# A norm over 64 rows as two products with a block of ones, in place of column sums and turns

## The chip, the cores and the metric

The kernel runs on one core of a Trainium2 chip. The metric is the device time of one execution in microseconds: 2410.14 us for the kernel before (median of 3 runs, 2409.24 to 2412.32). The core's engines work side by side, each on its own queue in order: TensorE (PE, matrix products into PSUM), VectorE (DVE), ScalarE (ACT), GpSimd (POOL) and SyncE (SP, which starts the DMAs).

## The reference

A decoder trunk of two layers on 512 positions of width 1024. A layer is: half a SwiGLU feed-forward step, a mixer, a cross-attention to a memory of 256 positions, another half feed-forward step. All in float32. The mixer has two groups of heads side by side: 8 stick-breaking attention heads of width 64, and 4 gated DeltaNet heads of width 128. What the change touches is the norm of each attention head's output, over its 64 channels:

```
sb = stick_breaking_attention(sq, sk, sv)             # (B, 8 heads, 512, 64)
sb = rms_norm(sb, sb_out_norm.reshape(8, 1, 64))      # x * rsqrt(mean(x*x) + 1e-6) * gain
...
return concatenate([sb, go]) @ w_out
```

## The kernel before

**Layout and precision.** Activations lie with channels on the 128 partitions and the 512 positions along the free axis. A product in the type fp32r takes one pass over its columns but rounds its operands, so the dense products are made of three: each operand is split into a high part (a cast on ACT, `split_act`, L177) and a low part (a subtraction on DVE, `split_low`, L182), and hi*hi, hi*lo and lo*hi are summed (`mm3`). Weights come as blocks of 128x1024 by SP's DMAs, four split blocks are held ahead. Products of plain fp32 operands are used where matrices are small.

**The threads of a mixer.** `mixer` writes four Python generators and `weave` merges them: the norm of the input, the DeltaNet heads (`mixer_gdn`, four heads one after another), the attention pairs (`mixer_sb`, `sb_pair` four times, two heads each), and the dense products (`mixer_dense`). The planner has a clock that grows with each matrix product by its estimated cost. A thread yields either a delay in ns, after which it may go on, or names of marks that must have been set and be due. Whenever several are ready, the first in the order above goes on, so the dense thread fills what the others leave. PE's instructions are issued exactly in the order so found; the other engines' order is made by the framework, with the DeltaNet heads' work at high priority. A delay costs nothing in itself: it only says how much other PE work is put between two steps, and PE waits if an operand is late.

**What orders the threads.** Dense projects pair p's queries, keys and values (`sb_project`) and sets the mark `sbp{p}`, due 2700 ns later; `sb_pair` p starts when it is due. Dense may start the projections of head 2 and 3 only after marks `q0` and `q1` (a head's recurrence has ended), those of pairs 2 and 3 only after `qk0` and `qk1` (a pair's scores of its second head are issued). After the fourth pair it projects the gates z, begins the memory's keys, and waits for `qk3`; further keys wait for `l3` (the last head's triangular solve) and `q3`; the output projection takes pair 3's operand when `sb3` is marked.

**A pair.** The values are turned (four 128x128 turns through PE, L776, with the identity) into PSUM bank b5, the only bank of the key "av". Then scores, weights and the values' products for its first head, 11000 ns of delay, and the same for its second. The values' products end in bank b5 too; ACT copies half of it (L956) and DVE adds (L957) into `o`, 128 rows of which the upper and lower 64 are one head each.

**The pair's norm.** ACT squares `o` (L959). After 3900 ns four fp32 products with the squares as the stationary operand and `bones` (128x2: ones on the rows of either head) as the moving one leave sums per position, 128 positions x 8 columns, in b5 (`col_sums`). DVE adds eps (L964), `rsqrt_log` makes exp(-0.5*ln x) on ACT and one Newton step on DVE, all on 8 columns, and DVE spreads each root over 64 columns (L968). After 4700 ns four turns bring this back to channels on partitions, again in b5, and DVE multiplies `o` by gain and root (L973). `sbp` of the next pair being due, the next pair's turns follow.

**The queries' copies.** `sb_project` keeps the queries' high part twice, on either half of the partitions; the second copy is a DVE copy of 64x512 (L851), twice a pair.

Of the kernel before, what the change touches and what calls it, by code (L numbers as in the profile page):

```python
# [19 lines left out]
F32 = mybir.dt.float32  # L20
F32R = mybir.dt.float32r
BF16 = mybir.dt.bfloat16
I32 = mybir.dt.int32
AF = mybir.ActivationFunctionType
ALU = mybir.AluOpType
PSUM = bass.MemoryType.PSUM

P = 128
# [12 lines left out]
EPS = 1e-6  # L41
# [8 lines left out]
G_F1, G_MX, G_XA, G_ME, G_F2, G_SB, G_GD, G_CV, G_AL, G_DT, G_LAYER = (  # L50
    0, 8, 16, 24, 32, 40, 44, 45, 93, 97, 101)
# [3 lines left out]
class Trunk:  # L55
# [59 lines left out]
    def mm(self, out, lhsT, rhs, **kw):  # L115
        r = rhs.dtype != F32
        n = 1
        for d in out.shape[1:]:
            n *= d
        self.clk += max(56.0 if rhs.dtype == BF16 else 107.0, n / 2.37) * (1 if r else 2)  # L120
        self.nc.tensor.matmul(out, lhsT, rhs, **kw)  # L121
# [711 lines left out]
    def sb_project(self, pair, x):  # L833


        nc = self.nc
        t4 = self.sb([P, 4, S], "qk", F32R, bufs=2)
        kk, qq = [t4[:, i, :] for i in range(2)], [t4[:, 2 + i, :] for i in range(2)]
        ql = self.ql[pair % 2]
        half = [slice(64 * i, 64 * i + 64) for i in range(2)]  # L840
        for j in range(2):
            ps = yield from self.project(x)
            tmp = self.slot("s12")
            nc.vector.scalar_tensor_tensor(out=tmp, in0=ps, scalar=0.125 if j == 0 else 1.0, in1=self.rb,
                                           op0=ALU.mult, op1=ALU.mult)
            dst = (qq, kk)[j]
            for i, r in enumerate(half):
                self.split_act(dst[i][r], tmp[r])
                self.split_low(ql[i][r] if j == 0 else kk[i][half[1 - i]], tmp[r], dst[i][r])
                if j == 0:  # L850
                    nc.vector.tensor_copy(qq[i][half[1 - i]], qq[i][r])  # L851
        if pair:
            yield (f"vt{pair - 1}",)
        ps = yield from self.project(x)
        self.vf = self.slot("s14")
        nc.vector.tensor_tensor(self.vf, ps, self.rb, op=ALU.mult)
        self.qk[pair] = kk, qq, ql
        self.mark(f"sbp{pair}", 2700.0)
# [6 lines left out]
    def sb_pair(self, layer, pair):  # L865


        nc = self.nc
        mm = self.mm
        t1s = ("s15", "s16", "s17")  # L870
        names = [f"s{i}" for i in range(22, 27)]
        yield (f"sbp{pair}",)
        b = self.bank("av", self.AV)
# [7 lines left out]
        kk, qq, ql = self.qk[pair]  # L881
# [54 lines left out]
        o = self.slot(("s0", "s1", "s13", "s37")[pair])  # L936
        for j in range(2):
# [7 lines left out]
            av = self.bank("av", self.AV)  # L945
            for s in range(NT):
                if j == 0 and s < 3:
                    yield from scores(1, s)
                    if s == 2:
# [5 lines left out]
            low = self.slot(self.turn("t1", t1s))  # L955
            nc.scalar.copy(low[own], av[other])  # L956
            nc.vector.tensor_tensor(o[own], av[own], low[own], op=ALU.add)  # L957
        sq = self.slot(self.turn("t1", t1s))
        nc.scalar.activation(sq, o, AF.Square)  # L959
        yield 3900.0  # L960
        b = self.bank("av", self.AV)
        self.col_sums(b, sq, self.bones, 2)
        ms = self.sb([P, 8], "sms", bufs=2)
        nc.vector.tensor_scalar(out=ms, in0=b[:, 0:8], scalar1=1.0 / 64, scalar2=EPS,  # L964
                                op0=ALU.mult, op1=ALU.add)
        r = self.rsqrt_log(ms, 8, "sn")
        wide = self.slot(self.turn("t1", t1s))
        nc.vector.tensor_copy(wide.rearrange("p (c d) -> p c d", d=64),  # L968
                              r.unsqueeze(2).to_broadcast([P, 8, 64]))
        yield 4700.0  # L970
        b = self.bank("av", self.AV)
        self.transposes(b, wide)
        nc.vector.scalar_tensor_tensor(out=o, in0=o, scalar=self.gain(layer, G_SB, pair), in1=b,  # L973
                                       op0=ALU.mult, op1=ALU.mult)
        self.sbo[pair] = o
        self.mark(f"sb{pair}", 17600.0)
# [601 lines left out]
```

## Time and profile before

| what | value |
|---|---|
| median of the runs | 2410.14 us |
| the profiled execution | 2411.89 us, its span 2410.1 us |
| mean granted TensorE clock | 0.996 |
| busy shares of the span | PE 99%, PE's weight loads 87%, DVE 73%, ACT 49%, POOL 0% |
| the two mixers | about 380 to 690 us and 1575 to 1880 us |

In the rows, PE is TensorE's products and PEld its weight loads, L121 is the line of `mm` (nearly all products) and L776 that of a turn. A matrix product's printed duration is modelled and overlaps the next one; the distance of two starts tells what one costs. What stands in square brackets is the engine's idle time just before the row and who ended it.

### The profile page before, as it was taken

The numbers are of one execution on the slowest core, as the hardware profiler recorded it, in microseconds if no ns is written. First come the engines' busy times: TensorE is split into PE (matmuls) and PEld (weight loads), VectorE is DVE, ScalarE is ACT, GpSimd is POOL, SyncE is SP. The second block draws the span as 40 slices with busy tenths as digits, with TensorE's granted clock in tenths as the row PEclk, the third lists the DMA queues.
The fourth block names the chain that finished last, engine by engine and source line by source line (L and its number), as shares of the span: only waits on it lengthen the run. The fifth ranks groups of instructions, "written<-read, shape, count | busy, mean of one in ns | idle before, by whom it ended". The sixth has DMA issues, their size and how long they took to land.

```text
span 2410.1 us, 35914 instructions
## 1 busy us (share of the span) xinstructions
PE 2376.2 (99%) x14320; PEld 2096.5 (87%) x14320; DVE 1763.6 (73%) x3121; ACT 1191.8 (49%) x2042; POOL 8.1 (0%) x19
## 2 busy tenths in 40 slices
PE   9999999999999999999999999999999999999998
PEld 7999987878888889898989999888788888899997
DVE  7767677888865577585786776689888655867765
ACT  5435355655644444353544444466666443444443
POOL 0000000000000000000000000000000000000000
PEclk9999999999999999999999999999999999999999
DMA  5324242112223123232323232311122322232322
GB/s 179 102 85 126 76 135 71 53 45 71 71 93 117 62 86 117 79 123 88 114 79 123 81 115 87 123 62 53 45 75 85 104 96 71 79 123 79 115 87 88
DMA packets 71416, 220.49 MB, mean 91 GB/s; under 512 B 7376, under 2 KB 18384, under 8 KB 71248
## 3 DMA queue, kind: packets, MB, share of 16 engines
q1 hardware_dynamic: 70816, 217.82, 27.8%
q8 instruction: 112, 1.84, 0.3%
q14 instruction: 56, 0.46, 0.1%
q10 hardware_dynamic: 432, 0.37, 0.1%
HBM read 216.07 MB, written 2.10 MB: 91 GB/s over the span
## 4 chain that ended last, share of the span: by engine, by line
PE 57%; DVE 3%; ACT 1%; issue 0%; DVEq 0%; ACTq 0%
PE b L121 57%; PE b L776 1%; DVE wlo L182 0%; DVE s L903 0%; DVE s L182 0%; DVE qkv L989 0%; DVE qk L182 0%; DVE s L705 0%; DVE s L905 0%; ACT whi L177 0%; ACT qk L177 0%; DVE qk L851 0%; DVE s L1086 0%; DVE s L1126 0%; DVE s L898 0%
## 5 line engine op out<-in xcount | busy, mean ns | idle before, releaser
L121 PE MATMUL b<-s,whi 128*128 128x256 f32 (+1 forms) x2818 | 648.9, 315 | 0.0
L177 ACT CAST whi<-wraw 128x1024 fp32r<-128x1024 f32 (+3 forms) x412 | 388.4, 954 | 478.2 <-PE b L121 408.1
L121 PE MATMUL b<-xh,whi 128*128 128x512 f32 (+1 forms) x1430 | 570.3, 399 | 1.4 <-DVE h L605 0.9
L182 DVE TENSOR_TENSOR wlo<-wraw,whi 128x1024 fp32r<-128x1024 f32 (+3 forms) x412 | 451.6, 1102 | 142.9 <-ACT whi L177 140.3
L121 PE MATMUL b<-xl,whi 128*128 128x512 f32 x1396 | 544.1, 390 | 0.2 <-DVE xl L311 0.2
L121 PEld LDWEIGHTS b<-s,whi 128*128 128x128 f32 x2818 | 468.5, 190 | 34.2
L121 PE MATMUL b<-s,wlo 128*128 128x256 f32 (+1 forms) x1426 | 449.9, 315 | 0.0
L121 PE MATMUL b<-xh,wlo 128*128 128x512 f32 x1106 | 432.4, 391 | 0.7 <-DVE wlo L182 0.7
L121 PEld LDWEIGHTS b<-xh,whi 128*128 128x128 f32 x1430 | 269.1, 188 | 51.8 <-ACT xh L179 1.3
L121 PEld LDWEIGHTS b<-xl,whi 128*128 128x128 f32 x1396 | 262.8, 188 | 49.3 <-DVE xl L182 0.9
L121 PEld LDWEIGHTS b<-s,wlo 128*128 128x128 f32 x1426 | 270.8, 190 | 17.7
L121 PEld LDWEIGHTS b<-xh,wlo 128*128 128x128 f32 x1106 | 207.6, 188 | 47.5 <-DVE wlo L182 2.6
L121 PE MATMUL b<-qk,whi 128*128 128x256 f32 (+1 forms) x1168 | 238.9, 289 | 0.0
L605 DVE SCALAR_TENSOR_TENSOR h<-b,h 128x512 f32<-128x512 f32 (+1 forms) x98 | 66.3, 680 | 173.5 <-PE b L121 173.5
L121 PEld LDWEIGHTS b<-qk,whi 128*128 128x128 f32 x1168 | 184.1, 191 | 2.4
L121 PE MATMUL b<-qkv,whi 128*128 128x256 f32 x900 | 180.0, 282 | 0.9 <-ACT s L562 0.9
L121 PE MATMUL b<-qk,wlo 128*128 128x256 f32 (+1 forms) x568 | 164.1, 289 | 0.0
L121 PEld LDWEIGHTS b<-qkv,whi 128*128 128x128 f32 x900 | 140.5, 190 | 1.3 <-ACT s L562 1.1
L177 ACT CAST whi<-vv 128x1024 fp32r<-128x1024 f32 x67 | 70.4, 1051 | 125.6 <-issue 71.4
L121 PE MATMUL b<-qkv,wlo 128*128 128x256 f32 x466 | 131.1, 281 | 0.0
L121 PE MATMUL b<-xl,wlo 128*128 128x512 f32 x290 | 112.4, 388 | 0.0
L121 PEld LDWEIGHTS b<-qk,wlo 128*128 128x128 f32 x568 | 108.5, 191 | 1.3
(300 smaller groups left out, 3283.5 us busy)
## 6 DMA issues: line engine op xcount, KB each, us to landing
wraw<-f2i SPq DMA_DIRECT2D x88, 512.0 KB, 3.6
wraw<-f1i SPq DMA_DIRECT2D x86, 512.0 KB, 3.7
wraw<-wi SPq DMA_DIRECT2D x56, 512.0 KB, 3.6
wraw<-f1o SPq DMA_DIRECT2D x32, 512.0 KB, 3.5
wraw<-xkv SPq DMA_DIRECT2D x32, 512.0 KB, 3.7
wraw<-f2o SPq DMA_DIRECT2D x32, 512.0 KB, 3.5
wraw<-wo SPq DMA_DIRECT2D x16, 512.0 KB, 3.7
wraw<-xq SPq DMA_DIRECT2D x16, 512.0 KB, 3.7
```

Of the source, the lines that this page charges most:

```text
L121: self.nc.tensor.matmul(out, lhsT, rhs, **kw)
L177: self.nc.scalar.copy(hi, src)
L182: return self.nc.vector.tensor_tensor(lo, src, hi.bitcast(F32), op=ALU.subtract)
L605: stt(out=h, in0=p, scalar=0.5, in1=h, op0=ALU.mult, op1=ALU.add)
L776: self.nc.tensor.transpose(out, src, self.ident[:src.shape[0], :src.shape[0]])
```

## The change

In `sb_project` the queries' second copy is made by ACT. In `sb_pair` the squares are split into a high and a low part like a dense operand. POOL spreads `bones` to a 128x128 matrix of ones on two diagonal 64x64 blocks (`heads`). After one delay of 5000 ns two fp32r products with `heads` as the stationary operand and the two parts as the moving one give the sum of each head's squares on all of its 64 rows at once, 128x512 in b5. Scaling and eps, logarithm, exponential and the Newton step then run on 128x512, and the last multiplication reads the root from SBUF. There are no turns back and no second delay. The seven new buffers come from the five slots s22 to s26 that the pair's weights rotate through ("sbs"), no longer from s15 to s17.

```diff
                 if j == 0:
-                    nc.vector.tensor_copy(qq[i][half[1 - i]], qq[i][r])
+                    nc.scalar.copy(qq[i][half[1 - i]], qq[i][r].bitcast(F32))
...
-        sq = self.slot(self.turn("t1", t1s))
+
+        room = lambda dt=F32: self.slot(self.turn("sbs", names), dt)
+        sq, hi, lo = room(), room(F32R), room(F32R)
         nc.scalar.activation(sq, o, AF.Square)
-        yield 3900.0
+        self.split_act(hi, sq)
+        heads = room(F32R)[:, :P]
+        nc.gpsimd.tensor_copy(heads.rearrange("p (a d) -> p a d", a=2), self.bones.unsqueeze(2).to_broadcast([P, 2, 64]))
+        self.split_low(lo, sq, hi)
+        yield 5000.0
         b = self.bank("av", self.AV)
-        self.col_sums(b, sq, self.bones, 2)
-        ms = self.sb([P, 8], "sms", bufs=2)
-        nc.vector.tensor_scalar(out=ms, in0=b[:, 0:8], scalar1=1.0 / 64, scalar2=EPS,
-                                op0=ALU.mult, op1=ALU.add)
-        r = self.rsqrt_log(ms, 8, "sn")
-        wide = self.slot(self.turn("t1", t1s))
-        nc.vector.tensor_copy(wide.rearrange("p (c d) -> p c d", d=64),
-                              r.unsqueeze(2).to_broadcast([P, 8, 64]))
-        yield 4700.0
-        b = self.bank("av", self.AV)
-        self.transposes(b, wide)
-        nc.vector.scalar_tensor_tensor(out=o, in0=o, scalar=self.gain(layer, G_SB, pair), in1=b,
+        mm(b, heads, hi, start=True, stop=False)
+        mm(b, heads, lo, start=False, stop=True)
+        ms, r, t = room(), room(), room()
+        nc.vector.tensor_scalar(out=ms, in0=b, scalar1=1.0 / 64, scalar2=EPS, op0=ALU.mult, op1=ALU.add)
+        nc.scalar.activation(r, ms, AF.Ln)
+        nc.scalar.activation(r, r, AF.Exp, scale=-0.5)
+        nc.vector.tensor_tensor(t, r, r, op=ALU.mult)
+        nc.vector.scalar_tensor_tensor(out=t, in0=t, scalar=-0.5, in1=ms, op0=ALU.mult, op1=ALU.mult)
+        nc.vector.scalar_tensor_tensor(out=r, in0=t, scalar=1.5, in1=r, op0=ALU.add, op1=ALU.mult)
+        nc.vector.scalar_tensor_tensor(out=o, in0=o, scalar=self.gain(layer, G_SB, pair), in1=r,
                                        op0=ALU.mult, op1=ALU.mult)
```

## Rows read from the trace of the kernel before

**Rows 1.** The page, busy time of each engine (share of the span, instructions).

```profile
PE 2376.2 (99%) x14320; PEld 2096.5 (87%) x14320; DVE 1763.6 (73%) x3121; ACT 1191.8 (49%) x2042; POOL 8.1 (0%) x19
```

**Rows 2.** PE's waits in the first mixer, 380 to 690: total us, times, longest.

```profile
PE b L121 <- DVE s L182: 2.8, 4, 1.1
...
PE b L121 <- ACT s L177: 0.2, 1, 0.2
```

**Rows 3.** Timeline of PE behind pair zero: start, us, engine, line, operation.

```profile
458.95 0.65 PE L121 MATMUL b<-s,vv 128*128 128x256 f32 x4
...
463.70 0.95 PE L121 MATMUL b<-cst,s 128*128 128x2 f32 x8
464.52 0.48 PE L121 MATMUL b<-xh,whi 128*128 128x512 f32 x1
464.83 0.40 PE L121 MATMUL b<-xl,whi 128*128 128x512 f32 x1
465.06 0.40 PE L121 MATMUL b<-xh,wlo 128*128 128x512 f32 x1
...
469.67 0.60 PE L776 MATMUL b<-cst,s 128*128 128x128 f32 x4
470.10 1.95 PE L121 MATMUL b<-qkv 128*128 128x128 f32 x16
471.89 0.60 PE L776 MATMUL b<-cst,s 128*128 128x128 f32 x4
```

**Rows 4.** Timeline of ACT and DVE, the same stretch.

```profile
461.30 0.63 ACT L959 ACTIVATE s<-s 128x512 f32<-128x512 f32 x1 [0.76 <-DVE s L957]
...
464.69 0.17 DVE L964 TENSOR_SCALAR sms<-b 128x8 f32<-128x8 f32 x1 [1.01 <-PE b L121]
...
466.14 0.68 DVE L1179 TENSOR_TENSOR s<-s,roy 128x512 f32<-128x512 f32 x1
...
467.28 0.42 DVE L968 COPY s<-sny 128x512 f32<-128x512 f32 x1
...
470.31 0.75 DVE L973 SCALAR_TENSOR_TENSOR s<-s,gn,b 128x512 f32<-128x512 f32 x1 [0.72 <-PE b L776]
```

**Rows 5.** Timeline, single instructions: a cast on POOL, a query copy on DVE.

```profile
14.98 0.31 POOL L166 CAST cb<-cst 128x128 bf16<-128x128 f32 x1 [14.53 <-DMA cst<-cst]
...
448.58 0.42 DVE L851 CAST qk<-qk 64x512 fp32r<-64x512 f32 x1
```

**Rows 6.** Stretches: us, then PE, PEld, DVE, ACT, POOL busy; PEclk, DMA share, GB/s.

```profile
460.00:480.00 20.00, 18.96 (x117) 15.93 (x115) 15.55 (x47) 12.74 (x37) 0.00 (x0) 1.00 0.16 53
500.00:520.00 20.00, 19.34 (x114) 16.05 (x114) 19.59 (x34) 14.71 (x22) 0.00 (x0) 1.00 0.16 50
600.00:650.00 50.00, 48.41 (x322) 43.49 (x320) 43.72 (x101) 34.15 (x68) 0.00 (x0) 0.93 0.16 54
1800.00:1850.00 50.00, 48.14 (x343) 43.58 (x342) 45.44 (x90) 32.92 (x56) 0.00 (x0) 0.97 0.20 64
```

**Rows 7.** Timeline of PE in pair three, first and second layer.

```profile
628.80 1.25 PE L776 MATMUL b<-cst,s 128*128 128x128 f32 x10
...
632.54 0.23 PE L121 MATMUL b<-cb 128*128 128x128 bf16 x1 [1.11 <-DVE s L182]
...
640.62 0.52 PE L121 MATMUL b<-s,whi 128*128 128x256 f32 x1
...
651.58 0.71 PE L121 MATMUL b<-yv,s 128*128 128x128 f32 x4 [0.28 <-DVE yv L1147]
...
1822.84 1.25 PE L776 MATMUL b<-cst,s 128*128 128x128 f32 x10
...
1844.21 0.71 PE L121 MATMUL b<-yv,s 128*128 128x128 f32 x4 [0.28 <-DVE yv L1147]
```

**Rows 8.** Timeline at the end of the second head's recurrence, first layer.

```profile
519.57 0.68 DVE L856 TENSOR_TENSOR s<-b,rb 128x512 f32<-128x512 f32 x1
...
528.03 0.49 PE L121 MATMUL b<-yv,s 128*128 128x128 f32 x2 [0.76 <-DVE yv L1147]
```

## The prediction

> **What bounds the kernel now.** I read the page first: PE is busy for 99% of the span, DVE for 73% [rows 1]. A busy PE is no proof that every microsecond counts, so I read PE's waits in the first mixer next: nine lines that add up to 8.8 us of about 300, the longest of them for DVE's low halves, 2.8 us [rows 2]. PE holds almost everything, and its order is fixed by the planner. Then I read the pair's tail instruction by instruction [rows 3, 4], then the places where PE does run dry [rows 7, 8].
>
> What those show: the four recurrent (DeltaNet) heads follow each other, and the dense thread may not pass certain marks of theirs. In the first layer the last dense product before such a mark is read by DVE at 519.57, and the head's last step comes at 528.03; in between PE only has pair one's values and the head's own chain, and waits on it, at the end for 0.76 us [rows 8]. The second place of this kind is dearer: dense is out when the ten turns start at 628.80, waits for pair three's second scores, and resumes at 640.62 [rows 7]. There the granted clock falls from 2.4 to 1.2 GHz behind a thin stretch that has a wait of 1.11 us in it: a mean of 0.93 over 50 us is 7 us at the low level, 0.97 in the second layer is 3 us [rows 6, 7]. From the same ten turns to the same head step, layer one takes 651.58-628.80 = 22.78 us, layer two 1844.21-1822.84 = 21.37 [rows 7]: 1.41 us for 4 us more at the low level, so 0.35 us each, 2.5 and 1.1 us for both. With the 1.11 us of waiting in each layer, this place costs 5.8 us in all. DVE is the tight neighbour: 19.59 of 20 us before the dry stretch, 15.55 just behind a pair's end [rows 6].
>
> **The change, part by part** (a pair occurs 4 times in each of 2 layers: 8 times).
>
> *PE, removed.* Four sums in fp32 (8 records) run from 463.70 to the next product's start at 464.52: 0.82 us. The switch back costs 0.08 more, as the first dense product then takes 0.31 and not the 0.23 that the following pair of starts shows (465.06-464.83). Four turns run from 469.67 to 470.10: 0.43. Together 1.33 us [rows 3].
> *PE, added.* Two 512-column products on operands written as fp32r, like the dense ones: 2 x 0.23 = 0.46. From the other side: if they ran like the fp32 sums, whose 8 records of two columns take 0.10 each, they would need two passes, 0.92. I take 0.46, as operands of the same kind stand in the dense rows. Saved: 0.87 a pair, 7.0 us in all (3.3 at the other end).
>
> *DVE.* Removed: four operations on 8 columns, 0.17 each, the spread copy 0.42 [rows 4], two query copies of 0.42 [rows 5]: 1.94. Added: low half, square of the root and two fused steps, each like the 0.68 of a 128x512 SBUF operation; and the scaling out of PSUM, for which no row stands: 0.42 (a copy from SBUF) to 0.75 (the fused operation with PSUM) [rows 4]. I take 0.7, nearest to the PSUM row. The last product now reads SBUF, -0.07. Net 3.42-2.01 = +1.4 a pair, 11.5 us in all. It lands behind the pair's end, where DVE has 4.5 us free in 20, while the query copies leave the stretch at 19.59 [rows 6]. I charge 1 us in all for PE waits that come from it; with no cover, all 11.5 us would show; the relieved stretch could in return give back as much as the 2.8 us of waits in each layer [rows 2].
> *ACT.* Added: the high half (0.6), two full-width functions at 0.63 in place of two on 8 columns, two query copies of no more than 0.63 [rows 4]: +3.1 a pair at most. ACT is at 14.71 of 20 us in the stretch of the copies and 12.74 behind the pair's end [rows 6]: nothing charged, up to 0.6 us a pair if a head's copy queues behind the high half.
> *POOL.* The block of ones spread to 128x128: a cast of that size took 0.31 [rows 5], POOL has nothing else then, and its slot is free when the last values end, some 5 us ahead of its use. Nothing; SP's queue is not touched.
>
> *The new wait ahead of the products.* Pair zero's squares start at 461.30 and take 0.63 [rows 4]; high half 0.6, low half 0.7: operands at about 463.4. The planner puts the products 5.0 us behind the last values, which start in the group at 458.95 and end near 459.6 [rows 3]: 464.6. Slack 1.2 us. PE as a whole would queue behind a late low half.
>
> *The bank.* The pair's sums, its turns back and the next pair's turns all use one PSUM bank. Before, 16 products of a head stand between the turns back (469.67) and the next pair's turns (471.89), so DVE's reading (470.31, 0.75) is covered [rows 3, 4]. Now the thread goes straight from the two products to the next pair's turns, if that pair's projections are marked. They then wait for: end of the products (0.4), DVE's scaling (0.7), two hand-overs of some 0.1, less the 0.23 of the last product: about 1.0, and up to 2.2 when a 1.2 us operation lies ahead on DVE. I take 1.2. It strikes surely between pairs zero and one, whose projections are long done; for the next two I expect the pair's end to come within 1 to 3 us of the projections' mark, so that something stands between, or PE is dry anyway. One a layer: +2.4 us.
> The Trainium skill speaks against this edit ("Perfetto Trace Analysis", Matmuls): independent groups should rotate through PSUM banks so that reading one out overlaps the next. The trace of before agrees as far as it goes: the reading was hidden, but by another thread's work. By that rule all six changes of pair pay, which is the slower rival below.
>
> *What moves.* A pair's end takes 5.0+0.5 us of the plan instead of 3.9+0.9+4.7+0.4, and the next pair starts some 6 us earlier; after three pairs it is about 16 to 18, as then the projections' mark limits it. Pair three's second scores, behind which dense resumed at 640.62 [rows 7], then end near 623 to 625, before dense is out. The dry place of 5.8 us then goes. But the heads' chain has not become shorter: dense next stops at the last head's solved and finished marks, and there PE is left with that chain alone, as at 519 to 528 [rows 8]. Bounds: nothing, or all 5.8; between them I count some four tenths as gained: -2.5.
>
> **Sum:** -7.0 (PE) +2.4 (bank) -2.5 (dry place) +1.0 (DVE) = -6.1 us on the profiled execution, 2411.89 to 2405.8. The median of the runs shown is 2410.14, 1.75 lower, which gives 2404.0.
>
> **Rivals.**
> *The heads' chain sets the pace.* Then work taken from PE only makes the dry stretches longer. For: the heads are one chain, with a dry stretch at its marks [rows 8]. Against: outside them PE runs with no gap for tens of us. It would leave the 1.25 us (0.82+0.43) of the last pair's tail in each layer, less the bank: 2410.1-2.5+2.4 = 2410, or 2407 with part of the rest.
> *The dry place goes entirely, clock included.* -7.0+2.4-5.8+1.0 = -9.4: 2400.7; down to 2396 if the relieved DVE returns half of its waits too.
> *The bank at every change of pair (slower).* Three waits a layer, six in all, in place of a covered reading. For: no yield stands between the products and the next turns; DVE is near full. Against: the projections' mark comes late for pairs two and three. At 2.2 us each, 13.2; with the DVE charge at 3 and nothing from the dry place: -7.0+13.2+3 = +9.2, 2419. It decides from a mean of 1.2 us over all six (7.0/6) for no gain at all.
> *It doesn't do what it says.* The products run at 0.92, or the operands come late each time: 3.3 saved less 2.4 of bank, 1 of DVE: 2410.
>
> **How the numbers follow.** A measurement of this kernel tells about 0.2%, 4.8 us, from no change: faster is below 2405.3, slower above 2415.0. Chances: the forecast (2401 to 2407.5, centre 2404) 0.43, of which 0.36 lies below the bound; heads' pace 0.24, of it 0.02 faster and 0.03 slower; dry place gone 0.12; bank every time 0.14, of it 0.12 slower; not as it says 0.07, of it 0.02 slower. Faster 0.50, same 0.33, slower 0.17. The range 2396 to 2413 leaves out a tenth on either side: below it only more than the whole dry place, above it the bank's rival and an uncovered DVE.
>
> **What would show it.** In the changed kernel's trace: two 512-column records a pair, 0.23 apart, in place of 8 short ones and four turns; PE's wait on DVE's scaling at the next pair's turns, about 1.2 us, once a layer; pair three's turns some 16 us earlier against its head; granted clock near 1.00 from 627 to 642. Wrong would be: waits at all six changes, low halves late at the products, DVE full behind a pair's end, or the half clock come back ahead of the last head's end.

## The result and the profile after

The changed kernel takes 2427.79 us (median of 3 runs, 2426.73 to 2429.57) against 2410.14: ratio 1.0073, 95% interval 1.006 to 1.0087, 17.65 us slower. 2404.0 was predicted, with 2396 to 2413 as its range.

The page of the changed kernel, the row that answers to [rows 1]:

```profile
span 2426.0 us, 35814 instructions
...
PE 2374.8 (98%) x14240; PEld 2065.4 (85%) x14240; DVE 1776.7 (73%) x3105; ACT 1200.8 (49%) x2064; POOL 14.9 (1%) x27
```

PE has 80 instructions less and is busy 1.4 us less, but the span grew by 15.9 us: PE's idle time (span less busy) went from 33.9 to 51.2 us. DVE's 13.1 us more are near the 11.5 of the sum. PE's waits in the first mixer of the changed kernel, 380 to 700 (total us, times, longest), beside [rows 2]:

```profile
PE b L121 <- DVE s L182: 3.2, 2, 1.7
PE b L121 <- DVE rhs L1145: 2.7, 3, 1.2
PE b L121 <- DVE yv L1151: 2.3, 6, 0.5
PE b L776 <- DVE s L971: 2.1, 2, 1.3
PE b L121 <- DVE s L1051: 2.0, 1, 2.0
PE b L121 <- DVE s L1121: 1.8, 2, 1.2
PE b L121 <- DVE qk L1257: 1.6, 1, 1.6
```

Fourteen lines now, 18.2 us in place of 8.8, and no line dominates: the head's solve (L1121) and recurrence (L1145, L1151), the eviction of its scaled keys (L1051), the low halves, the new bank wait (L971). Nearly all end on DVE.

The timeline of PE in the changed kernel, which answers to [rows 3, 7, 8]:

```profile
459.84 0.60 PE L776 MATMUL b<-cst,qkv 128*128 128x128 f32 x4
...
462.14 0.62 PE L121 MATMUL b<-s,s 128*128 128x512 f32 x2
464.04 0.66 PE L776 MATMUL b<-cst,s 128*128 128x128 f32 x4 [1.27 <-DVE s L971]
...
526.77 1.10 PE L121 MATMUL b<-s,s 128*128 128x512 f32 x2
528.66 0.66 PE L776 MATMUL b<-cst,s 128*128 128x128 f32 x4 [0.78 <-DVE s L971]
...
531.75 0.62 PE L776 MATMUL b<-cst,qkv 128*128 128x128 f32 x4
...
542.13 2.05 PE L121 MATMUL b<-qkv 128*128 128x128 f32 x16 [2.00 <-DVE s L1051]
...
593.51 0.60 PE L776 MATMUL b<-cst,s 128*128 128x128 f32 x4
...
655.36 1.39 PE L121 MATMUL b<-s,s 128*128 128x512 f32 x9 [1.65 <-DVE s L182]
657.96 2.04 PE L121 MATMUL b<-s,s 128*128 128x128 f32 x8 [1.21 <-DVE s L1121]
```

The two products of a norm are there (x2), and the next pair's turns come at 464.04, 528.66 and 593.51: 8, 10 and 16 us earlier than before, about as forecast. The third has no bank wait, the first two have one. And the third head (turns out of `qkv`) is late: 531.75 where before had 528.58, although the head ahead of it began 2.3 us earlier.

Stretches of the changed kernel, columns as in [rows 6]:

```profile
460.00:480.00 20.00, 18.65 (x105) 14.75 (x102) 18.66 (x50) 13.82 (x39) 0.00 (x0) 1.00 0.01 1
500.00:520.00 20.00, 18.18 (x108) 15.34 (x108) 19.23 (x33) 12.55 (x20) 0.00 (x0) 1.00 0.15 49
600.00:650.00 50.00, 48.42 (x335) 43.37 (x334) 47.41 (x107) 34.55 (x73) 0.42 (x1) 1.00 0.27 90
650.00:680.00 30.00, 24.04 (x151) 21.69 (x149) 19.09 (x39) 10.07 (x24) 0.00 (x0) 0.83 0.21 71
```

The last of these stretches in the kernel before:

```profile
650.00:680.00 30.00, 29.60 (x211) 26.97 (x210) 21.20 (x45) 13.23 (x30) 0.00 (x0) 1.00 0.43 141
```

The old dry place is gone (clock 1.00 from 600 to 650, where it was 0.93), and a worse one stands at 650 to 680: the last head is alone, and PE is without work for 6 us. It waits 0.59, 1.65 and 1.21 us between 651 and 658, and again, up to 1.19 us at a time, between 668 and 675; the clock is at its low level, 1.2 GHz, from about 658 to 661 and from about 671.5 to 678.5 (a mean of 0.83 over the 30). Before had PE busy for 29.60 us and the clock at 1.00 there. DVE at 460 to 480 has gone from 15.55 to 18.66 of 20 us.

**The balance.** I measure a mixer from the first head's first turns to the eight turns of the output projection. "Idle" is that time less PE's busy time in it; "low" is the time at 1.2 GHz, twice the missing share of the granted clock summed over stretches of 1 us; "work" is busy less half of "low" (half, as in after a 256-column product took 0.21 us at 660.23, at the low level, and 0.12 at 661.41, at the high one). Both mixers together, profiled executions, us:

| kernel | mixers | work | idle | low | rest of the span |
|---|---|---|---|---|---|
| before | 575.0 | 553.6 | 16.3 | 10.2 | 1835.1 |
| after | 596.3 | 548.9 | 35.5 | 23.9 | 1829.7 |

The mixers lose 21.3 us: -4.7 of PE's work, +19.2 of idle time, +6.8 for 13.7 us more at the low level (half of each is lost). The rest of the span gains 5.4, where neither kernel's instructions differ (last section). "Work" is a rough figure: kernels with one and the same queue on PE differ in it by up to 3.8 us (after, e3, e6 and e7 below: 547.4 to 551.2).

### The profile page after: what moved, and what is told of

Its sections match the earlier page's. It is cut to its first block, busy times and chain, and to the rows that moved or that the text cites. A ratio compares the mean times of both kernels' runs of the same rounds, so it can differ in the third digit from the quotient of the medians.

```text
span 2426.0 us, 35814 instructions
## 1 busy us (share of the span) xinstructions
PE 2374.8 (98%) x14240; PEld 2065.4 (85%) x14240; DVE 1776.7 (73%) x3105; ACT 1200.8 (49%) x2064; POOL 14.9 (1%) x27
## 4 chain that ended last, share of the span: by engine, by line
PE 89%; DVE 7%; ACT 2%; issue 1%; DMA 1%; SPq 0%; ACTq 0%; POOL 0%; DVEq 0%
PE b L121 87%; PE b L776 1%; DVE s L903 1%; DVE wlo L182 1%; ACT whi L177 1%; DVE s L898 1%; DVE s L905 0%; DMA wraw<-f1i 0%; DVE s L182 0%; DMA s<-csr 0%; DVE qkv L993 0%; DVE s L957 0%; DVE s L1090 0%; ACT qk L177 0%; DVE s L1102 0%
## 5 line engine op out<-in xcount | busy, mean ns | idle before, releaser
L121 PE MATMUL b<-s,whi 128*128 128x256 f32 (+1 forms) x2818 | 641.2, 314 | 0.0
L121 PE MATMUL b<-xh,whi 128*128 128x512 f32 (+1 forms) x1430 | 576.4, 403 | 1.5 <-DVE h L605 0.9
L121 PE MATMUL b<-xl,whi 128*128 128x512 f32 x1396 | 551.4, 395 | 0.2 <-DVE xl L311 0.2
L121 PEld LDWEIGHTS b<-s,whi 128*128 128x128 f32 x2818 | 461.0, 188 | 39.0
L121 PEld LDWEIGHTS b<-xh,wlo 128*128 128x128 f32 x1106 | 207.7, 188 | 51.2 <-DVE wlo L182 1.6
L121 PE MATMUL b<-qk,whi 128*128 128x256 f32 (+1 forms) x1168 | 231.8, 283 | 0.0
```

## Experiments

The comparisons that follow have this balance each; "ratio" is the time against the kernel before on the same chip, whose medians lay between 2410.9 and 2412.1.

| run | time, ratio [95%] | mixers | work | idle | low |
|---|---|---|---|---|---|
| e1_start_as_before | 2432.18, 1.0085 [1.007, 1.01] | 602.6 | 546.1 | 36.0 | 41.0 |
| e2_bank_covered | 2422.68, 1.0047 [1.003, 1.0064] | 589.7 | 549.0 | 32.2 | 17.1 |
| e3_copy_on_dve | 2432.74, 1.0088 [1.0073, 1.0103] | 599.2 | 551.2 | 37.8 | 20.5 |
| e4_copy_alone | 2408.07, 0.9988 [0.9979, 0.9997] | 571.3 | 552.3 | 15.6 | 6.8 |
| e5_before_more_dve | 2412.05, 1.0005 [0.9996, 1.0014] | 573.2 | 554.6 | 18.7 | 0.0 |
| e6_no_newton | 2421.24, 1.004 [1.0026, 1.0054] | 588.3 | 547.4 | 30.7 | 20.5 |
| e7_root_on_act | 2429.71, 1.0077 [1.0062, 1.0092] | 586.1 | 548.2 | 29.3 | 17.1 |
| e8_root_on_act_late | 2430.34, 1.0079 [1.0064, 1.0094] | 583.8 | 547.9 | 29.1 | 13.7 |
| e9_order_kept | 2409.89, 0.9992 [0.9983, 1.0001] | 577.3 | 551.9 | 22.0 | 6.8 |
| e10_order_kept_late | 2431.67, 1.0084 [1.0069, 1.0099] | 600.0 | 552.1 | 41.0 | 13.7 |
| e11_before_minus_850 | 2428.73, 1.0071 [1.0056, 1.0086] | 591.6 | 550.5 | 30.9 | 20.5 |
| e12_before_plus_850 | 2436.57, 1.01 [1.0083, 1.0117] | 600.5 | 557.1 | 33.1 | 20.5 |
| e13_after_minus_850 | 2437.19, 1.0105 [1.009, 1.012] | 605.6 | 546.7 | 38.4 | 40.9 |
| e14_after_plus_850 | 2431.88, 1.0082 [1.0067, 1.0097] | 600.4 | 547.0 | 36.3 | 34.2 |
| e15_order_kept_dve_copy | 2412.45, 1.0001 [0.9991, 1.001] | 581.0 | 552.7 | 23.2 | 10.2 |
| e16_start_in_between | 2440.65, 1.012 [1.0105, 1.0135] | 606.5 | 545.6 | 42.1 | 37.5 |
| e17_order_kept_no_newton | 2402.45, 0.9962 [0.9947, 0.9976] | 570.1 | 549.1 | 17.6 | 6.8 |
| e18_order_kept_late_no_newton | 2433.01, 1.0088 [1.0071, 1.0105] | 600.0 | 550.0 | 32.9 | 34.2 |

A balance is that of one execution, and the time at the low level differs between executions of one kernel: e8's four had mean granted clocks of 0.991 to 0.996, by which I estimate some 24 us at the low level between them. e6, e7, e8, e17 and e18 leave the Newton step out of the computation. Five groups have one and the same order of PE's queue each: before, e4 and e5; after, e3, e6 and e7; e1 and e8; e9, e15 and e17; e10 and e18. e9, e15 and e17 have before's order with the products in place of the sums; in e10 and e18 they stand in place of the turns back.

**The early start and the bank.** Both add a delay behind the last multiplication, so that the next pair starts later:

```diff
         self.mark(f"sb{pair}", 17600.0)
+        yield 4450.0      # e1;  e2: 1300.0
```

e1: 

> After, with one more delay of 4450 ns at the pair's end, so that the next pair starts where it did before (5.0+0.4+4.45 = 9.9 us of the plan, as 3.9+0.9+4.7+0.4). Theory A (the earlier start costs: it brings pair work into stretches where the heads' chain then runs at its slower, filled pace, and moves the dry stretch to the last head, where the clock falls): 2402 to 2410. Rival B (the wait for the bank alone): the bank is read by then, so 2427.8 less the four waits of 4.1 us: about 2423. Rival C (the norm's heavier DVE work): 2425 to 2428, no change.

e2: 

> After, with a delay of only 1300 ns at the pair's end: dense products stand between the norm's products and the next pair's turns while DVE reads the bank. Theory A: most of the loss stays, 2420 to 2426, as the pairs still start some 3 to 5 us early each. Rival B: the waits of 1.27 and 0.78 us in each layer are gone and with them the loss that follows from them, 2412 to 2423. Rival C: 2425 to 2428.

e1 was slower still, so the loss doesn't need the early start: the bank wait is gone in e1 and other waits stand in its place (low halves 7.5 us in three waits of the first mixer). In e2 the bank wait is gone too, and 5.1 us come back of the 17.65; as e2's delay changes PE's order as well, that isn't the price of the bank alone. The wait is real, and most of the loss stays without it.

**The copy.** e3 is the changed kernel with the queries' copy back on DVE, e4 the kernel before with the copy alone on ACT.

```diff
-                    nc.vector.tensor_copy(qq[i][half[1 - i]], qq[i][r])
+                    nc.scalar.copy(qq[i][half[1 - i]], qq[i][r].bitcast(F32))
```

e3: 

> After, with the queries' second copy back on DVE, so that the norm's edit stands alone. Theory A: the copy edit is worth some 2 to 6 us (after was 1.9 us ahead when the first head started and 2.8 us at the first pair's turns): 2429 to 2434. Rival C (DVE load is the cause): 13.4 us of DVE work more, and slower by a good part of it: 2434 to 2441. If the copy on ACT were the cause of the loss: under 2420.

e4: 

> Before, with the queries' second copy on ACT and nothing else of the change. Theory A: a gain of 2 to 6 us, 2404 to 2408, the lead that the trace of after shows ahead of the first norm. Rival (the copy slows ACT's work for the heads): 2412 or more.

The copy is worth 5 us in the changed kernel and about 3 in the kernel before; it is the half of the change that helps. The loss is the norm's. (e3's expectation counts 13.4 us of DVE work; there are 16 copies of 0.42 us, 6.7 in all.)

**DVE's work.** e5 puts four more multiplications of 128x512 into each pair of the kernel before, between the sums and the turns back (21.8 us in all). e6 takes the three Newton operations out of the changed kernel; e7 also lets the logarithm read the bank with scale and bias, four DVE operations less; e8 is e7 with the delay of e1.

```diff
+        for _ in range(4):                                             # e5, in before
+            nc.vector.tensor_tensor(wide, o, o, op=ALU.mult)
...
-        nc.vector.tensor_tensor(t, r, r, op=ALU.mult)                  # e6, e7, e8
-        nc.vector.scalar_tensor_tensor(out=t, in0=t, scalar=-0.5, in1=ms, op0=ALU.mult, op1=ALU.mult)
-        nc.vector.scalar_tensor_tensor(out=r, in0=t, scalar=1.5, in1=r, op0=ALU.add, op1=ALU.mult)
...
+        nc.scalar.activation(r, b, AF.Ln, scale=1.0 / 64, bias=self.eps)   # e7, e8
```

e5: 

> Before, with four more DVE multiplications of 128x512 (0.68 us each) into the buffer of the spread root, ahead of the spread copy; their result is overwritten. That is 2.7 us of DVE work more a pair, 21.8 in all, at the place where the changed norm has its full-width steps; PE's work and plan stay as before. Theory D (the norm's DVE work, packed behind a pair's end, delays the next head's and pair's DVE steps; PE waits and its clock falls): 2418 to 2432. Rival A' (the loss comes from PE's order, that is from what the planner puts where): 2408 to 2414.

e6: 

> After, without the Newton step on the root (left out: the refinement; the root is the one of exp and ln). Three DVE operations of 0.69 us less a pair, 16.5 us in all. Theory D: half of the loss or more comes back, 2410 to 2420. Rival A': the plan of PE is the same to the instruction, 2424 to 2428.

e7: 

> After, without the Newton step, and with scaling and eps inside the logarithm, which ACT reads from the bank itself: DVE has only the low half and the last multiplication left, 4 operations of 0.69 us less a pair, 22 us in all. Theory D: 2404 to 2416, with the wait for the bank (now on ACT) still there. Rival A': 2422 to 2428.

e8: 

> The kernel with the root on ACT alone, and the next pair started where it was before (one more delay of 4450 ns). Theory D: light on DVE, no wait for the bank, starts as before: 2400 to 2410, the 7 us of PE work saved at last. Rival A': with the starts as before but the loss still there (the after kernel with this delay had 2432): above 2424.

By their times e5, e7 and e8 seemed to say that DVE's work doesn't matter. The balance says otherwise. The rest of the span is 1841.5 us in e7 and e8 and 1830 to 1831 in every other kernel with the new norm: 11 us that have nothing to do with a pair (3 of them stand ahead of the first mixer; these two have one more constant in SBUF, and why that costs stays open). In the mixers alone, with the same order on PE, three operations less give 8.0 us (after to e6) and four give 10.2 (after to e7). From e1 to e8 the profiled executions differ by 18.8 us, but they are e1's slowest and e8's fastest, and 27.3 us at the low level lie between them; by the medians, less the 11 us elsewhere, four operations give about 13. In e5 the idle time rose by 2.4 us. Its profiled execution hides that, with no time at the low level in the mixers; by the medians of its ten executions e5 is 1.1 us slower than before, which is within the noise. So DVE's work can cost, and how much depends on where it stands; yet e7, with 5.8 us less on DVE in the mixers than before has, is still 11 us slower there.

**The order of PE's queue.** e9 does the changed kernel's operations, with delays and clock steps such that everything around them stands in before's order; e10 the same with the products where the turns back stood; e15 is e9 with the copy on DVE. e11 and e12 are the kernel before with its second delay 0.85 us of plan shorter or longer, e13 and e14 the changed kernel with its one delay so, e16 lies between e2 and e1.

```diff
-        yield 5000.0
+        yield 3900.0                     # e9 (e10: the products behind the second delay)
+        due = self.clk + 856.0
         b = self.bank("av", self.AV)
         mm(b, heads, hi, start=True, stop=False)
         mm(b, heads, lo, start=False, stop=True)
+        self.clk = due
...
+        yield 4700.0
+        self.clk += 428.0
         self.mark(f"sb{pair}", 17600.0)
```
```diff
-        yield 4700.0
+        yield 3850.0                     # e11 in before;  e12: 5550.0
...
-        yield 5000.0
+        yield 4150.0                     # e13 in after;  e14: 5850.0
```

e9: 

> After, in the order of before: the two products stand where the four sums stood (3900 ns behind the last values), a delay of 4700 ns follows, and the planner's clock is advanced by what the sums and turns had counted (856 and 428 ns), so that everything behind is put in the same place as before; the turns back are simply missing. Theory A' (the order of PE's queue is the cause, not the operations): 2400 to 2408, that is the saved 7 us and the copy on ACT, less waits for a low half that comes up to 1 us late at 3900 ns. Rival W (the new operations cost, wherever they stand): 2420 to 2432.

e10: 

> The same with the two products where the turns back stood (3900+0.9+4700 ns behind the last values): no low half can be late, but the bank is read just ahead of the next pair's turns, behind 16 products of a head. Theory A': 2400 to 2408. Rival W: 2420 to 2432.

e11: 

> Before, with the second delay of a pair's end at 3850 instead of 4700 ns and no other change: the same work, and the planner's clock shifted by as much as the change's cheaper products shift it. Theory A', in the form that the order of before is a good one among many, and small shifts of the plan alone cost 10 to 20 us: 2418 to 2430. Theory W: 2409 to 2413.

e12: 

> Before, with the second delay at 5550 instead of 4700 ns and no other change: the next pair starts 0.85 us later by the plan. Theory A' (small shifts cost either way): 2414 to 2430. If only an earlier start costs: 2407 to 2412, or a gain. Theory W: 2409 to 2413.

e13: 

> The changed kernel with its one delay at 4150 in place of 5000: the products 0.85 us of plan earlier, nothing else. Theory O (the order of PE's queue sets the time; the changed kernel's order is one draw of many): it moves by 5 us or more against the changed kernel's 2427.8, to either side, with PE's idle time and the half-clock time moving and PE's work at full clock the same. Theory C (the full-width norm is what costs, in any order but the old one): 2424 to 2432. The bank's wait on the scaling should stay at 1 to 3 us a layer, and low halves may be late at the products.

e14: 

> The changed kernel with its one delay at 5850: the products 0.85 us of plan later, nothing else. Theory O: again 5 us or more from 2427.8, to either side, in the range 2405 to 2440. Theory C: 2424 to 2432.

e15: 

> The changed norm in the order of the kernel before (as in the order-kept kernel, 2409.9), with the queries' second copy back on DVE: the norm alone. If the two parts add up (copy alone -3.1, both -2.2), it comes to +0.9 against the kernel before, 2411 to 2415. If the copy on the scalar engine is needed to make room on DVE for the new norm, as the 5 us that it was worth in the changed kernel hint: +3 or more, 2415 to 2418.

e16: 

> The changed kernel with 2600 of plan between the root and the next pair's start (nothing: 2427.8, 1300: 2422.7, 4450: 2432.2). Theory O: no monotonous line through these; anything from 2405 to 2435. If the free bank is the gain and a later start the loss, it lies between, 2424 to 2430. No wait on the scaling at the next pair's turns in either case.

This is the cause. With before's order the change costs no time in total (0.9992, or 1.0001 without the copy); from e9 to after lie 17.9 us by the medians (0.0081 by the ratios, 19.5), with the same operations. As e9 has them too, neither the new buffers in s22 to s26 nor POOL's copy is the cause by itself. And the kernel before, with not one operation changed, loses 17 and 25 us when one of its delays moves by 0.85 us of plan. The changed kernel scatters as well, from 2422.7 to 2440.7 over the six orders tried beside the kept ones, with all its operations, and no order other than before's, of either kernel, came below 2421.

Two limits belong to this. The total of e9 hides something: its mixers are, in the profiled executions, 2.3 us longer than before's, and e15's, which have the new norm without the copy, 6.0 us longer, with more idle time (22.0 and 23.2 against 16.3); the rest of the span, where nothing was changed, is 4 to 5 us shorter and covers that. And e10 shows that before's order around the norm isn't enough: with the two products moved to the place of the turns back it loses 20 us.

Several expectations missed. e1, e7, e12, e16 and e18 came out slower than every range given, e6 and e9 between their two; e10 lay in the range of the rival by which the operations cost wherever they stand, which e9 excludes, and e14 in that of the full-width norm.

Where the order costs is read from the first mixer, heads 1 to 3 together (us): from a head's first turns to its sixteen products with `qkv`, from there to its second turns, from there to the next head's first turns (for the last: to the output projection's).

| kernel | start | middle | recurrence |
|---|---|---|---|
| before | 23.5 | 35.1 | 162.2 |
| after | 29.2 | 35.3 | 166.4 |
| e9 | 23.1 | 35.7 | 161.8 |
| e10 | 22.5 | 37.0 | 173.6 |
| e11 | 27.4 | 34.0 | 166.0 |
| e12 | 24.3 | 46.1 | 163.6 |

It is not one place. In e12 it is the bank. PE's timeline of e12: sixteen products, turns back, and straight behind them the next pair's turns:

```profile
543.45 1.95 PE L121 MATMUL b<-qkv 128*128 128x128 f32 x16
545.23 0.60 PE L776 MATMUL b<-cst,s 128*128 128x128 f32 x4
548.89 0.66 PE L776 MATMUL b<-cst,s 128*128 128x128 f32 x4 [3.07 <-DVE s L973]
```

In before the same sixteen stand between the two groups of turns [rows 3] and cover DVE's reading; 0.85 us of plan later they don't, and PE waits 8.1 us a layer for the bank, 16.3 in all; its idle time is 16.8 us above before's. In the changed kernel it is the head's start. The same stretch, first PE and DVE of before (start, us, engine, line), then DVE of after:

```profile
528.58 0.60 PE L776 MATMUL b<-cst,qkv 128*128 128x128 f32 x4
...
535.27 0.68 DVE L1047 TENSOR_TENSOR s<-b,ke 128x512 f32<-128x512 f32 x1
536.69 0.75 DVE L973 SCALAR_TENSOR_TENSOR s<-s,gn,b 128x512 f32<-128x512 f32 x1 [0.73 <-PE b L776]
```

```profile
531.49 0.69 DVE L975 SCALAR_TENSOR_TENSOR s<-s,s 128x512 f32<-128x512 f32 x1
532.22 0.69 DVE L976 SCALAR_TENSOR_TENSOR s<-s,s 128x512 f32<-128x512 f32 x1
...
532.90 0.68 DVE L898 SCALAR_TENSOR_TENSOR s<-b,s 128x512 f32<-128x512 f32 x1
...
533.57 0.74 DVE L977 SCALAR_TENSOR_TENSOR s<-s,gn,s 128x512 f32<-128x512 f32 x1
...
534.38 1.22 DVE L903 TENSOR_TENSOR_SCAN s<-cst,s 128x512 f32<-128x512 f32 x1
...
536.10 0.69 DVE L905 TENSOR_TENSOR s<-b,s 128x512 f32<-128x512 f32 x1
...
541.40 0.68 DVE L1051 TENSOR_TENSOR s<-b,ke 128x512 f32<-128x512 f32 x1
```

DVE starts on the head's scaled keys (L1047, L1051) 6.69 us behind its first turns (528.58) before, and 9.65 behind them (531.75) after. In between DVE now has the root's last steps and the scores of the pair that started 10 us earlier (L898, L903, L905), which before came behind the head's sixteen products. From 530.6 to 545 it has no gap, and PE waits 2.00 us at 542.13.

**The Newton step in the kept order.** e17 and e18 are e9 and e10 without the three operations of e6.

e17: 

> The changed norm in the order of the kernel before (2409.9), without the Newton step: three 128x512 operations of 0.68 us less on DVE for each pair, 16 us of DVE's work in all; this leaves the Newton step out of the computation. If DVE's work costs nothing in the old order, as the run with 21.8 us more of it shows: 2407 to 2411. If it is DVE's work that eats the 7 us of PE work saved there: 2400 to 2405.

e18: 

> The kept order with the two products at the place of the turns back (2431.7), without the Newton step; PE's queue is the same. If the loss there is DVE's full-width root meeting the next pair's scores and the head's steps, as in the changed order (8 us of both mixers come back with the same three operations): 2418 to 2425. If only the lateness of the root counts and not DVE's work: it comes 2 us earlier for the last multiplication alone, and the time stays at 2428 to 2432.

e17 is faster than both kernels, 0.9962 (0.9947 to 0.9976), though without the Newton step. The page of e9, and of e17:

```profile
span 2408.1 us, 35776 instructions
...
PE 2368.8 (98%) x14240; PEld 2058.2 (85%) x14240; DVE 1776.0 (74%) x3105; ACT 1202.2 (50%) x2064; POOL 10.5 (0%) x27
```

```profile
span 2400.5 us, 35759 instructions
...
PE 2366.1 (99%) x14240; PEld 2059.7 (86%) x14240; DVE 1762.7 (73%) x3081; ACT 1203.8 (50%) x2066; POOL 10.7 (0%) x27
```

In the mixers idle time falls from 22.0 in e9 to 17.6, near before's 16.3. So even in before's order DVE's work was not covered: three operations, 16 us of DVE, cost 7 us. The stretch that was gapless on DVE in the changed kernel, in e17:

```profile
527.00:545.00 18.00, 18.00 (x102) 14.88 (x101) 16.16 (x43) 12.88 (x33) 0.00 (x0) 1.00 0.09 30
```

in after, and in e9, which has all of after's operations:

```profile
527.00:545.00 18.00, 14.75 (x86) 11.78 (x85) 16.23 (x44) 13.54 (x40) 0.00 (x0) 1.00 0.01 2
```

```profile
527.00:545.00 18.00, 17.67 (x100) 14.29 (x99) 16.93 (x44) 12.44 (x36) 0.00 (x0) 1.00 0.10 30
```

DVE is as full in all three (16.16, 16.23 and 16.93 of 18 us); PE has no gap in e17, 3.25 us in after and 0.33 in e9. In e9 DVE starts on the head's scaled keys 6.95 us behind the head's first turns (526.81), close to before's 6.69:

```profile
533.76 0.68 DVE L1055 TENSOR_TENSOR s<-b,ke 128x512 f32<-128x512 f32 x1
```

At this place DVE's load doesn't tell PE's idle time: what counts is what DVE does first. In e18 the time did not come back: idle time fell by 8.1 us, but 20.5 us more at the low level took 10 of it. Why e10's order loses 20 us stays open; its starts are as good as before's, its waits are the convolutions' evictions (3.8 us in the first mixer) and pair three's operand at the output projection (2.9 in one wait).

## Why the prediction was wrong

**PE's work, -7.0.** About right by the rows: two products took 0.46 (463.12 to 463.58 in e2) to 0.55 us (591.59 to 592.14 in after) in place of 1.33, 6.2 to 7.0 in all. The mixers' "work" fell by 4.7, too rough a figure to confirm it (ten kernels with the whole new norm lie at 545.6 to 552.7, five with the old one at 550.5 to 557.1).

**The bank, +2.4.** The mechanism was right, the count off: two of three changes of pair a layer, 1.27 and 0.78 us, 4.1 us in all; e2, without them and in another order, was 5.1 us faster. The Trainium skill's rule that independent groups should rotate through PSUM banks ("Perfetto Trace Analysis", Matmuls) agrees with these rows. The slower rival built on it priced six waits at 2.2 us; they were four at 1.0, and did not decide. In e12 the same wait, six times, 16.3 us in all, did.

**DVE, +1.0.** Mis-sized. Its added work was about right (13.1 us against 11.5; eight times its own 1.41 is 11.3), its cover was not. I read DVE's free time off sums over 20 us [rows 6], where 4.5 us were free in one stretch. The three Newton operations alone cost 6.6 us in the changed kernel and 7.4 in the kept order.

**What moves, -2.5. This is the step that failed.** The moves came about as forecast: pairs 8, 10 and 16 us earlier (the forecast says some 6 for the first, though its own plan, 5.5 in place of 9.9, gives 4.4), the old dry place gone. I counted the moves as a gain of some four tenths of that place, with "nothing, or all 5.8" as bounds, and so took the rest of the order for neutral. A new order is not neutral: the pairs' earlier scores came onto DVE at the next head's start, the dense work was used up earlier, and the last head was left alone from 650 on, at clock 0.83. From e9 to after, with the same operations, the order costs 17.9 us, all of the loss, where my bounds excluded any. Two of the signs that I had named as wrong came: DVE full behind a pair's end (18.66 of 20 us), and the half clock ahead of the last head's end.

**The rivals.** "The heads' chain sets the pace" (2407 to 2410) is what the kept order gave, 2409.9: with the order as before, idle time took what PE's work gave, though by DVE's work and not only by the chain. That the number fits is partly luck, as the unchanged rest of the span gave 4.3 us. Its sign to look for was there in [rows 8]: PE waiting for the head's own last step. None of the rivals had a new order that costs by itself.

**The parts' sum.** The change in before's order: -2.2 us by the medians of that comparison, of which the copy gives 3.1 alone. The norm by itself is then about +1, as e15 shows (1.0001); in the mixers it is +6.0, the copy -3.7 and both +2.3.

## What to carry to other kernels

Where one in-order queue is merged from several threads by a planner, an edit that changes a step's planned length or removes a delay is two edits: the work, and a new order. Price them apart by holding the old order (pad the planner's clock), and learn the order's own spread by moving one delay in the unchanged kernel; here that spread (17 and 25 us for 0.85 us of plan) was larger than everything that the work could give. When the times of such runs disagree, split them first into PE's work, idle time and time at the low clock, and by stage: for e7 and e8, and for e9 and e15, the total hid what the stage showed.

## What was not expected

The rest of the span differs by 5 us between kernels whose instructions there are the same. In the first feed-forward step, 100 to 300 us, grouped rows of PE by line and form (busy us, mean ns of one), before and after:

```profile
L121 PE MATMUL b<-s,whi 128*128 128x256 f32 x315 | 59.6, 283 | 0.0
L121 PE MATMUL b<-qk,whi 128*128 128x256 f32 x182 | 35.6, 283 | 0.0
L121 PE MATMUL b<-xh,whi 128*128 128x512 f32 x72 | 28.0, 389 | 0.0
```

```profile
L121 PE MATMUL b<-s,whi 128*128 128x256 f32 x321 | 58.8, 278 | 0.0
L121 PE MATMUL b<-qk,whi 128*128 128x256 f32 x184 | 34.7, 276 | 0.0
L121 PE MATMUL b<-xh,whi 128*128 128x512 f32 x72 | 28.5, 396 | 0.0
```

Products of 256 columns are 5 to 7 ns shorter in the changed kernel, those of 512 columns 7 ns longer, long before the first norm; these durations are modelled, and whether they make the difference isn't shown. Outside the mixers kernels with the old norm take 1834.5 to 1835.4 us, those with the new one 1830 to 1831, and those with one more constant 1841. The cause was not tried.
